# Projections with channels in rows from normed activations, and longer runs of half-array products, in a hybrid decoder layer

## The chip, the cores and the metric

The kernel runs on one core of one Trainium2 chip. The metric is device time in microseconds (us) for one execution, of the slowest core (here the only one). Times of a kernel are given as the median of several runs. One execution is recorded by the hardware profiler, and all rows of a profile come from that one.

The engines are TensorE (PE in the rows, its weight loads PEld), VectorE (DVE), ScalarE (ACT), GpSimd (POOL) and SyncE (SP), which here issues the DMAs. TensorE multiplies a stationary operand (128x128 at most) with a moving one and writes PSUM, which has eight banks of 512 fp32 columns in 128 partitions.

## The reference, cut to what matters

One decoder layer on 256 tokens of width 1024, in fp32:

```python
h = rms_norm(x, ln1_g)
q, k, v, z, xbc, dt, gate_a, gate_b = split(h @ w_in)          # 1024 -> 10272
y_a = attention(head_norm(q), head_norm(k), v) @ w_o_attn        # 16 heads of 64, causal in one block
xbc = silu(causal_conv(xbc))                                     # depthwise, 4 taps along the tokens
y   = ssd(xbc, softplus(dt + dt_bias)) + d_skip * xs             # 32 heads of 64, 4 groups, 2 chunks of 128
y_b = (group_rms_norm(y * silu(z)) * norm_g) @ w_o_ssm
x  += (sigmoid(gate_a) * y_a + sigmoid(gate_b) * y_b) @ w_out
h2  = rms_norm(x, ln2_g)
g, u = split(h2 @ w_gate_up)                                     # 2 x 2816
x  += (silu(g) * u) @ w_down
x  += (p @ w_ple_proj) * sigmoid(rms_norm(x, ln3_g) @ w_ple_gate)
```

## The kernel before, in words

**Precision.** TensorE multiplies in a format that rounds fp32 (`F32R`). Each weight tile and each activation is split into a rounded part and the rest: `wh` by ScalarE, `wl = raw - wh` by VectorE (`split_w`, L263), likewise `ah` and `al`. A product is the sum of `ah wh + ah wl + al wh`.

**Panels.** A panel is 512 output columns for all 256 tokens. `Panel.step` (L348) makes, for one slice of 128 of the inner dimension and one half of the tokens, three matmuls whose stationary operand is the activation (128 channels x 128 tokens) and whose moving operand is 512 columns of the weight. Tokens come out in the partitions, in two PSUM banks (tag `g`, four banks). A panel of inner dimension 1024 has 48 matmuls. `PANELS` lists the panels of the input projection in their order. `yb` stands for a group of the SSM's output projection (`ssm_out`, L846). The activations are `g1 * x` without the factor 1/rms; that factor, `rstd1`, is applied to each panel's result.

**After a panel.** xbc and z are wanted with channels in the partitions. `evac_xbc` (L482) and `evac_z` (L516) therefore scale the result into SBUF, transpose it with TensorE (eight 128x128 transposes for a panel, L192), and then take the convolution or the tanh. Gate and up are computed as eleven panels of 256 gate and 256 up columns; `evac_gu` (L996) takes the sigmoid and the products, and `ff_task` (L1006) transposes the result (four transposes) and splits it for the down projection.

**SSM and attention.** `ssm_task` (L591) goes through four groups of eight heads, in two units of four heads. `seg` makes the decays, `out_` (L664) the diagonal products: matmuls with 64 stationary columns, two of which run in the two halves of the array (`halves`, L176). `off` adds what the first chunk passes to the second, `ssm_finish` (L717) gates and norms. `attention_task` (L746) goes through eight pairs of heads: `scores`, `transp`, `values`.

**Residuals.** `Residual.take` (L954) adds a panel to the residual stream, transposes and splits the sum, and makes 1/rms beside that. For gate/up the 1/rms is applied at the end, in `evac_gu`.

**Order.** The order on TensorE is written out: `queue` (L156) makes every instruction follow the last main matmul, and `Filler` slips the small tasks between the steps of panels. A task says how many modelled nanoseconds it waits before its next part (`LAG`, by step). On the other engines the order follows ranks (`prio`): weights (`w`) come before evacuations (`ev`), these before the rest (`bg`). The DMAs of the weights stand on SP's queue, 512 KB each, with four raw, three `wh` and six `wl` tiles.

Of the kernel before, what the change touches and what calls it, by code (L numbers as in the profile page):

```python
# [10 lines left out]
F32 = mybir.dt.float32  # L11
# [24 lines left out]
    ('xbc', 0, 5120),  # L36
    ('xbc', 5, 7680),
    ('xbc', 1, 5632),
    ('xbc', 2, 6144),
    ('xbc', 3, 6656),  # L40
    ('k', 0, 1024),
    ('q', 0, 0),
    ('z', 0, 3072),
    ('z', 1, 3584),
    ('gb', 0, 9248),
    ('yb', 0, None),
    ('yb', 1, None),
    ('q', 1, 512),
    ('v', 0, 2048),
    ('z', 3, 4608),  # L50
    ('k', 1, 1536),
    ('z', 2, 4096),
    ('gb', 1, 9760),
    ('v', 1, 2560),
    ('yb', 2, None),
    ('yb', 3, None),
    ('ga', 1, 8736),
    ('ga', 0, 8224),
]
NFF = 11  # L60

# [5 lines left out]

LAG = {
    "dt": 9198, "dt.t": 3823, "dt.e": 24762, "dt.low": 2074, "dt.end": 6965, "xbc": 3815, "xbc.t": 1507,
    "xbc.end": 7967, "z": 7477, "z.t": 2878, "z.end": 2196, "qk": 21856, "qk.t": 1263, "qk.end": 1856,  # L70
    "v": 3215, "cb": 0, "rows": 538, "prep": 3126, "seg": 492, "seg.next": 11553, "out": 13590,
    "out.xdt": 4839, "out.end": 90, "off": 3340, "off.end": 560, "finish": 6082, "finish.ones": 3453,
    "sc": 6834, "sc.tr": 2218, "tr": 0, "tr.val": 759, "val": 2876, "val.end": 3654, "m": 1401, "res": 4378,
    "ff": 1875, "ff.end": 1668,
# [34 lines left out]
def tile_layer(ctx: ExitStack, tc: tile.TileContext, head, xk, pt, vec, w_dt, w_big, w_dn2, w_pp, out):  # L109
    nc = tc.nc  # L110

    counters = {"w": 0, "ev": 100000, "bg": 200000, "mm": 400000}
# [15 lines left out]

    def nm(s):
        uid[0] += 1  # L130
        return f"{s}_{uid[0]}"
# [4 lines left out]
    def s2(shape, dt=F32):  # L136
        return sb.tile([P] + shape, dt, tag="s2", bufs=8, name=nm("s2"))

    def tiny(shape, dt=F32):
        return sb.tile([P] + shape, dt, tag="tiny", bufs=12, name=nm("tiny"))  # L140
# [50 lines left out]
    def transpose(o, i):  # L191
        queue(nc.tensor.transpose(o, i, ident[: i.shape[0], : i.shape[0]]).ins, False)  # L192
        fill.now += 107.0


    with prio("w"):
# [7 lines left out]
        for _ in range(7):  # L204
# [3 lines left out]
        ones = const.tile([P, 1], F32, name="ones")  # L208
        nc.vector.memset(ones, 1.0)
# [45 lines left out]
    def w_tiles():  # L255
        return (sb.tile([P, 2, 512], F32, tag="raw", bufs=4, name=nm("raw")),
                sb.tile([P, 2, 512], F32R, tag="wh", bufs=3, name=nm("wh")),
                sb.tile([P, 2, 512], F32R, tag="wl", bufs=6, name=nm("wl")))

    def split_w(tiles, js=slice(0, 2)):  # L260
        raw, wh, wl = (t[:, js] for t in tiles)
# [7 lines left out]
    def load(src, nk):  # L269

        with prio("w"):
            parts = []
            for k in range(0, nk, 2):
                tiles = w_tiles()
                nc.sync.dma_start(tiles[0], src[:, k : k + 2])
                split_w(tiles)
                parts += parts_of(tiles)
        return parts

    def load_first():  # L280

        parts = [[], []]
        with prio("w"):
            load_head(x0)
            for k in (0, 2):
                tiles = [w_tiles() for _ in range(2)]
                for j in range(2):
                    if k + j:
                        load_x(k + j, 1)
                    for b in range(2):  # L290
                        load_head(tiles[b][0][:, j])
                for j in range(2):
                    split_h(k + j)
                    for b in range(2):
                        tc.keep_in_program_order(split_w(tiles[b], slice(j, j + 1)))
# [15 lines left out]
    def next_chunk():  # L311
        c = w_big[chunk_no[0]]
        chunk_no[0] += 1
        return load(c, 4)
# [12 lines left out]
    class Panel:  # L327
# [3 lines left out]
        def __init__(self, cut=False):  # L331
# [15 lines left out]

        def step(self, piece, part, act_, last):  # L348
            tt, c, ps = piece
            ah, al = act_  # L350
# [10 lines left out]
    def rstd_of(dst, ss, scale, eps=EPS):  # L361
        t = tiny([ss.shape[-1]])
        nc.vector.tensor_scalar(t, ss, scale, eps, op0=ALU.mult, op1=ALU.add)  # L363
# [4 lines left out]
    rstd1 = const.tile([P, 2], F32, name="rstd1")  # L368
    hrstd1 = const.tile([P, 2], F32, name="hrstd1")
    eps1 = const.tile([P, 2], F32, name="eps1")  # L370

    def x_stats():
        with prio("bg"):
# [12 lines left out]
            nc.vector.tensor_scalar(hrstd1, rstd1, 0.5, None, op0=ALU.mult)  # L386

# [11 lines left out]
    def dt_task():  # L399
# [7 lines left out]
        yield fill.now + LAG["dt"]  # L407
# [12 lines left out]
        yield fill.now + LAG["dt.t"]  # L420
        with prio("bg"):
            pt_ = pb([512])
            u = tiny([2, 32])
# [6 lines left out]
            e = tiny([2, 32])  # L430
            stt(e, u, -1.0, u, op0=ALU.mult, op1=ALU.max)
            act(e, e, AF.Exp, scale=-1.0)
            s = tiny([2, 32])
# [3 lines left out]
            sq = tiny([2, 32])  # L437
            nc.vector.tensor_mul(sq, s, s)
            pol = tiny([2, 32])
# [7 lines left out]
            ea = tiny([32])  # L447
            act(ea, v[:, V_AL : V_AL + 32], AF.Exp)
            af = tiny([2, 32])
# [4 lines left out]
        yield fill.now + LAG["dt.e"]  # L454
        with prio("bg"):
# [7 lines left out]
            low = tiny([2, 32])  # L463
            nc.vector.tensor_scalar(low, pe[:, 0:2], -80.0, 80.0, op0=ALU.max, op1=ALU.min)
            el = tiny([2, 32])
# [4 lines left out]
        yield fill.now + LAG["dt.low"]  # L470
# [5 lines left out]
        yield fill.now + LAG["dt.end"]  # L476
# [3 lines left out]
    xsT, zsT, bc, qk_t, v_of, gates = {}, {}, {}, {}, {}, {}  # L480

    def evac_xbc(i, pan):  # L482
# [6 lines left out]
        yield fill.now + LAG["xbc"]  # L489
        c = s4([4, T])  # L490
        for jj in range(2):
            with prio("bg"):
# [4 lines left out]
                for j in range(2):  # L497
                    ct = 4 * i + 2 * jj + j
                    cw = [v[:, V_CW + 4 * ct + m : V_CW + 4 * ct + m + 1] for m in range(4)]
                    cc = c[:, 2 * jj + j]  # L500
                    act(cc, pu[:, j], AF.Identity, scale=cw[3], bias=v[:, V_CB + ct : V_CB + ct + 1])
                    for sft in (1, 2, 3):
                        stt(cc[:, sft:], pu[:, j, : T - sft], cw[3 - sft], cc[:, sft:], op0=ALU.mult, op1=ALU.add)  # L503
            yield fill.now + LAG["xbc.t"]
        with prio("bg"):

            th = s4([4, T])
            act(th, c, AF.Tanh, scale=0.5)
# [609 lines left out]
```

## Time and profile before

| | us |
|---|---|
| median of 3 runs (601.69 to 602.17) | 602.16 |
| the profiled execution, whole | 601.78 |
| its span, first to last instruction | 600.0 |
| PE busy | 593.8 |
| PE weight loads busy | 484.2 |
| DVE busy | 423.7 |
| ACT busy | 338.5 |
| POOL busy | 38.5 |
| input projection with SSM and attention, to the first `w_o_attn` panel | about 332 |
| gate and up, eleven panels | about 391 to 519 |

Busy times can overlap between engines. A row of the groups gives line, engine, operation, output and inputs by name, shapes, the count, then the busy time in us, the mean of one in ns, and the idle time before. L170 is the helper through which all matmuls go, L192 that of the transposes, L151 that of ACT's operations; so the operands' names tell them apart. `g` is a PSUM tile of a panel, `pb` one of the small tasks, `s` any tile in SBUF. A matmul's duration in a row contains its way through the array and overlaps with the next one.

### The profile page before, as it was taken

The page shows a single profiled execution, that of the slowest core. Times are in us where ns is not written, and L with a number is a line of the kernel's source. Part 1 is how long each engine was busy: PE and PEld are TensorE (multiplying, and loading weights), DVE is VectorE, ACT ScalarE, POOL GpSimd, SP SyncE. Part 2 cuts the span into 40 slices and gives each one's busy share as a digit, 9 for nine tenths or more (in the row PEclk, how much of TensorE's full clock was granted, in tenths as well). Part 3 has the DMA queues.
Part 4 walks back from the last instruction along what each step waited for, and adds up shares of the span by engine and source line. Part 5 has one row for each costly group of instructions (what it writes and reads, how often), then busy time and mean ns, then how long its engine had stood idle before and what let it go on. Part 6 is the DMA issues. An engine that isn't in the chain of part 4 may idle for free.

```text
span 600.0 us, 8135 instructions
## 1 busy us (share of the span) xinstructions
PE 593.8 (99%) x2961; PEld 484.2 (81%) x2961; DVE 423.7 (71%) x667; ACT 338.5 (56%) x512; POOL 38.5 (6%) x47
## 2 busy tenths in 40 slices
PE   9999999999999999999999999999999999999997
PEld 7888888787777878887777788888888888888886
DVE  5689999978997765677865575756756666646465
ACT  6766666556774545476646444755544544445353
POOL 2000103412010111101000000000000000000000
PEclk9999999999999999999999999999999999999999
DMA  8845644543444445655555475556555565555641
GB/s 303 320 141 167 208 143 142 176 137 113 138 135 144 143 156 162 194 167 158 160 159 163 140 234 186 186 165 203 170 202 185 163 202 189 184 188 183 196 147 70
DMA packets 31048, 103.88 MB, mean 173 GB/s; under 512 B 3552, under 2 KB 4640, under 8 KB 31008
## 3 DMA queue, kind: packets, MB, share of 16 engines
q1 hardware_dynamic: 31008, 103.36, 53.3%
q8 instruction: 23, 0.38, 0.3%
q14 instruction: 17, 0.14, 0.1%
HBM read 102.23 MB, written 1.05 MB: 172 GB/s over the span
## 4 chain that ended last, share of the span: by engine, by line
PE 97%; DVE 1%; ACT 0%; DMA 0%; issue 0%; SPq 0%; ACTq 0%
PE g L170 85%; PE pb L170 6%; PE pb L192 5%; DMA raw<-in_head 0%; DVE s L733 0%; ACT wh L151 0%; DVE s L641 0%; ACT s L151 0%; DVE wl L263 0%; DVE s L768 0%; DVE s L646 0%; DVE s L725 0%; DVE s L1043 0%; DVE s L1044 0%; DVE s L765 0%
## 5 line engine op out<-in xcount | busy, mean ns | idle before, releaser
L170 PE MATMUL g<-wh,s 128*128 128x512 f32 x1504 | 486.7, 395 | 0.1
L170 PEld LDWEIGHTS g<-wh,s 128*128 128x128 f32 x1504 | 282.1, 188 | 59.1 <-issue 1.9
L263 DVE TENSOR_TENSOR wl<-raw,wh 128x1024 fp32r<-128x1024 f32 (+1 forms) x192 | 230.2, 1201 | 130.3 <-ACT wh L151 128.0
L151 ACT ACTIVATE wh<-raw 128x1024 fp32r<-128x1024 f32 (+1 forms) x192 | 199.7, 1042 | 176.2 <-PE g L170 151.6
L170 PE MATMUL g<-wl,s 128*128 128x512 f32 x752 | 294.8, 392 | 0.0
L170 PEld LDWEIGHTS g<-wl,s 128*128 128x128 f32 x752 | 141.6, 188 | 28.2 <-issue 1.0
L151 ACT ACTIVATE s<-pb 128x512 f32<-128x512 f32 (+4 forms) x64 | 33.6, 543 | 30.6 <-PE pb L192 16.1
L192 PEld LDWEIGHTS pb<-ident,s 128*128 128x128 f32 x302 | 37.9, 140 | 11.4 <-issue 0.9
L192 PE MATMUL pb<-ident,s 128*128 128x128 f32 x302 | 47.1, 272 | 0.0
L151 ACT ACTIVATE s<-g,rstd 128x512 f32<-128x512 f32 (+1 forms) x50 | 28.5, 583 | 20.8 <-PE g L170 19.1
L503 DVE SCALAR_TENSOR_TENSOR s<-pb,vecs,s 128x255 f32<-128x255 f32 (+2 forms) x72 | 32.0, 474 | 1.8 <-ACT s L151 1.6
L170 PE MATMUL pb<-s,s 128*64 128x128 f32 (+6 forms) x328 | 32.6, 304 | 0.4 <-ACT s L151 0.4
L151 ACT ACTIVATE s<-pb,vecs 128x256 f32<-128x256 f32 (+2 forms) x48 | 25.9, 549 | 10.9 <-PE pb L192 5.0
L170 PEld LDWEIGHTS pb<-s,s 128*64 128x64 f32 (+2 forms) x328 | 23.1, 154 | 9.9 <-issue 4.7
L364 POOL TENSOR_TENSOR rstd<-tiny,mhalf 128x2 f32<-128x2 f32 x3 | 2.3, 762 | 314.4 <-DVE tiny L363 295.3
L151 ACT ACTIVATE s<-s 128x512 f32<-128x512 f32 (+3 forms) x24 | 19.0, 792 | 5.0 <-DVE s L958 4.0
L554 POOL TENSOR_TENSOR tiny<-tiny,mhalf 128x8 f32<-128x8 f32 x8 | 16.0, 1994 | 73.2 <-DVE tiny L552 73.2
L618 POOL TENSOR_SCALAR_AFFINE_SELECT rr<-a_h 128x512 fp32r<-128x512 f32 x16 | 13.6, 860 | 100.7 <-PE pb L170 56.9
L151 ACT ACTIVATE s<-s,tiny 128x128 f32<-128x128 f32 (+1 forms) x32 | 14.2, 445 | 6.4 <-DVE tiny L771 6.4
L1002 DVE SCALAR_TENSOR_TENSOR s<-g,rstd,s 128x256 f32<-128x256 f32 x22 | 10.6, 481 | 7.5 <-ACT s L151 7.5
L659 DVE TENSOR_TENSOR s<-s,s 128x512 f32<-128x512 f32 x16 | 11.9, 747 | 0.3 <-ACT s L151 0.3
L1003 DVE SCALAR_TENSOR_TENSOR s<-g,rstd,s 128x256 f32<-128x256 f32 x22 | 10.6, 484 | 0.7
(120 smaller groups left out, 235.6 us busy)
## 6 DMA issues: line engine op xcount, KB each, us to landing
raw<-in_w_big SPq DMA_DIRECT2D x176, 512.0 KB
raw<-in_head SPq DMA_DIRECT2D x8, 256.0 KB
raw<-in_head SPq DMA_DIRECT2D x4, 512.0 KB
s<-in_xk SPq DMA_DIRECT2D x4, 512.0 KB
raw<-in_w_pp SPq DMA_DIRECT2D x2, 512.0 KB
raw<-in_w_dn SPq DMA_DIRECT2D x2, 512.0 KB
out<-s SPq DMA_DIRECT2D x3, 256.0 KB
xraw<-in_head SPq DMA_DIRECT2D x2, 256.0 KB
```

The source lines that it names most:

```text
L151: return nc.scalar.activation(o, i, f, **kw)
L170: ins = nc.tensor.matmul(o, lhsT, rhs, start=start, stop=stop).ins
L192: queue(nc.tensor.transpose(o, i, ident[: i.shape[0], : i.shape[0]]).ins, False)
L263: nc.vector.tensor_sub(wl, raw, wh.bitcast(F32))
L364: nc.gpsimd.tensor_tensor(dst, t, mhalf[:, : ss.shape[-1]], op=ALU.pow)
L503: stt(cc[:, sft:], pu[:, j, : T - sft], cw[3 - sft], cc[:, sft:], op0=ALU.mult, op1=ALU.add)
L554: nc.gpsimd.tensor_tensor(f, ms, mhalf, op=ALU.pow)
L618: nc.gpsimd.affine_select(r, bcast(a_h[:, c, h0 : h0 + 4].bitcast(F32), P), pattern=[[0, 4], [1, P]], compare_op=ALU.is_ge, fill=0.0, base ...
L659: nc.vector.tensor_tensor(m, m, cbm[:, g, c].unsqueeze(1).to_broadcast([P, 4, P]), op=ALU.mult)
L1002: stt(t[:, tt], pan.ps[tt][:, :T], r, t[:, tt], op0=ALU.mult, op1=ALU.mult)
L1003: stt(t[:, tt], pan.ps[tt][:, T:], r, t[:, tt], op0=ALU.mult, op1=ALU.mult)
```

## The change

- **Channels in rows.** From the sixth panel on (`NORMED`), xbc and z panels (`BY_ROWS`, eight of them) and all of gate/up make the weight the stationary operand and the activations the moving one, so that channels come out in the partitions. *Narrow* blocks take three matmuls with 256 columns, *wide* ones (`WIDE`, and all of gate/up) take one with 512 columns, `wh` against `[ah | al]`, and one with 256, `wl` against `ah`; their two halves are then added. The weights' layout in memory follows.
- **Normed activations.** `norm_rows` makes `g1 * x / rms` once and splits it again; 1/rms is spread over the partitions by a product of ones and a diagonal matrix. Panels from the sixth on need no factor after them.
- **Residual before gate/up.** The sum is scaled by 1/rms before it is transposed and split; these steps have the new highest rank (`hot`), and the transposes stand between the products of the p projection.
- **Runs of half-array products.** `out_` takes all eight heads of a group in one run; three of the four value products of attention follow directly on the next pair's scores.
- **The start.** The first weight load is two halves; `open` orders the first products by what is there; one warming product fewer.
- **Also.** Another panel order; a waiting time for each single use of a step; four `wh` and five `wl` tiles, more small tiles; the group norm's sum over channels by transposes and ACT's accumulator; small steps of 1/rms on POOL.

```diff
 PANELS = [
-    xbc4 xbc0 xbc5 xbc1 xbc2 xbc3 k0 q0 z0 z1 gb0 yb0 yb1 q1 v0 z3 k1 z2 gb1 v1 yb2 yb3 ga1 ga0
+    xbc4 xbc0 k0 gb0 v0 xbc5 q0 xbc1 z0 xbc2 z3 xbc3 z1 yb0 q1 k1 yb1 z2 v1 yb2 ga1 gb1 ga0 yb3
 ]
+NORMED = 5
+BY_ROWS = [kind in ('xbc', 'z') and n >= NORMED for n, (kind, _, _) in enumerate(PANELS)]
+WIDE = [('z', 0), ('z', 1), ('z', 2), ('xbc', 5), ('xbc', 3)]
...
+    def rows_step(ps, tiles, k, acts_, wide):
+        wh, wl = (x.rearrange("p a n -> p (a n)")[:, k * P : k * P + P] for x in tiles[1:])
+        ah, al, both = acts_[k]
+        if wide:
+            if k == 7:
+                mm(ps[:, :T], wl, ah, False, False, main=True)
+            mm(ps, wh, both, k == 0, k == 7, main=True)
+            if k < 7:
+                mm(ps[:, :T], wl, ah, False, False, main=True)
+        else:
+            mm(ps, wh, ah, k == 0, False, main=True)
+            mm(ps, wh, al, False, False, main=True)
+            mm(ps, wl, ah, False, k == 7, main=True)
+        fill.step()
...
+    def norm_rows():
+            pr = pb([T])
+            mm(pr, ones, rdiag.rearrange("p a t -> p (a t)"), True, True)
+            for k in range(0, 8, 2):
+                h32 = s2([2, T])
+                both = s4([2, 2, T], F32R)
+                for j in range(2):
+                    stt(h32[:, j], xk_, g1[:, k + j : k + j + 1], pr, op0=ALU.mult, op1=ALU.mult)
+                act(both[:, :, 0], h32)
+                nc.vector.tensor_sub(both[:, :, 1], h32, both[:, :, 0].bitcast(F32))
...
+                    for k in range(8):
+                        rows_step(ps if wide else ps[:, j], w, k, h_n, wide)
+                    if wide:
+                            act(u[:, j], ps[:, T:])
+                            nc.vector.tensor_add(u[:, j], ps[:, :T], u[:, j])
+                evac_rows(kind, i, jj, u if wide else ps, to)
...
-        def out_(g, qd):
-                yds = [pb([2, P]) for _ in range(2)]
+        def out_(g):
+                yds = [pb([2, 2, P]) for _ in range(2)]
                 halves(
-                    for j in range(2) for c in range(2) for hf in range(2))
+                    for qd in (1, 0) for j in range(2) for c in range(2) for hf in range(2))
...
-        def scores(p):
+        def scores(p, also=None):
+                vals, finish = values(*also) if also else ([], None)
-                halves(
+                halves([
-                    for hf in range(2))
+                    for hf in (1, 0)] + vals)
...
 class Residual, take:
-            fill.spawn(split_t(...), 0)
+            if not self.normed:
+                fill.spawn(split_t(...), 0)
-            with prio("bg"):
+            with prio("hot" if self.normed and n == 1 else "bg"):
                     act(junk, b[:, tt], AF.Square, accum_out=self.ss[:, tt, n : n + 1])
+                        nc.gpsimd.tensor_add(sss, self.ss[:, tt, 0:1], self.ss[:, tt, 1:2])
+                        rstd_of(self.dst[:, tt : tt + 1], sss, 1.0 / 1024, on=nc.gpsimd)
+                            scaled = act(self.toks[nn][tt], self.base[nn][:, tt], scale=self.dst[:, tt : tt + 1])
...
+                pan.step(pc, parts[k], (p_h[:, k], p_l[:, k]), k == 1)
+                if 4 * n + 2 * tt + k >= 4:
+                    res2.split(*ready.pop(0))
...
+    def gate_up(n, pg, pu):
+            act(u[:, 0], pg[:, T:])
+            nc.vector.tensor_add(u[:, 0], pg[:, :T], u[:, 0])
+            act(f[:, 0], u[:, 0], AF.Sigmoid)
+            nc.vector.tensor_mul(f[:, 0], f[:, 0], u[:, 0])
+            act(u[:, 1], pu[:, T:])
+            nc.vector.tensor_add(u[:, 1], pu[:, :T], u[:, 1])
+            nc.vector.tensor_mul(f[:, 0], f[:, 0], u[:, 1])
+            act(fh, f[:, 0])
+            nc.vector.tensor_sub(fl, f[:, 0], fh.bitcast(F32))
+    for n in range(2 * NFF):
+        tiles = load_tiles(next_src(), 4, None if n else res2.scaled)
+        pss = [psg.tile([P, 512], F32, tag="g", name=nm("g")) for _ in range(2)]
+            for ps, w in zip(pss, tiles):
+                for k in range(8):
+                    rows_step(ps, w, k, h2, True)
+        gate_up(n, *pss)
```

More of the change, by code (lines that the diff above doesn't have):

```diff
@@ L189, in mm3, with transpose @@
         mm(o, ll, rh, False, stop)
-    def transpose(o, i):
-        queue(nc.tensor.transpose(o, i, ident[: i.shape[0], : i.shape[0]]).ins, False)
+    def transpose(o, i, main=False):
+        queue(nc.tensor.transpose(o, i, ident[: i.shape[0], : i.shape[0]]).ins, main)
         fill.now += 107.0
@@ L275, in load, with cuts @@
                 nc.sync.dma_start(tiles[0], src[:, k : k + 2])
-                split_w(tiles)
-                parts += parts_of(tiles)
-        return parts
+                rounded = split_w(tiles)
+                if behind is not None and k + 2 == nk:
+                    follow(rounded.ins, behind)
+                yield tiles
+    def load(src, nk):
+        return [part for tiles in load_tiles(src, nk) for part in parts_of(tiles)]
+    def cuts(k, b):
+        return [WHOLE] if k or b else HALVES
     def load_first():
@@ L488, in evac_xbc @@
                 tok.append(t)
-        yield fill.now + LAG["xbc"]
+        yield fill.now + lag("xbc")
         c = s4([4, T])
@@ new lines, in evac_xbc, with evac_rows, end_rows @@
+            yield fill.now + lag("xbc.t")
+        yield from silu_xbc(i, c)
+    def evac_rows(kind, i, jj, ps, to):
+        with prio("ev"):
+            if kind == "xbc":
+                conv(i, to, jj, ps)
+            else:
+                zz = to[:, 2 * jj : 2 * jj + 2]
+                act(zz, ps, AF.Tanh, scale=0.5)
+                stt(zz, zz, 1.0, ps, op0=ALU.add, op1=ALU.mult)
+    def end_rows(kind, i, to):
+        if kind == "xbc":
+            yield from silu_xbc(i, to)
+        else:
+            yield fill.now + lag("z.end")
+            zsT[i] = to
@@ L813, in values, with finish, wait_values @@
                     prods += [(pa[rows_of[hf], i, P:T], vt[:, 1, cols[hf]], t1[:, hf], False, True) for hf in range(2)]
-                halves(prods)
-                act(ah, pa)
-                nc.vector.tensor_sub(al, pa, ah.bitcast(F32))
-        for n in range(10):
+            def finish():
+                with prio("bg"):
+                    act(ah, pa)
+                    nc.vector.tensor_sub(al, pa, ah.bitcast(F32))
+            return prods, finish
+        def wait_values(p):
+            while p[0] not in v_of:
+                yield fill.now + 500
+            yield tm["t", p] + lag("tr.val")
+        for n in range(9):
             if n < 8:
```

472 lines of the change are left out of this document (273 added, 199 removed).

## The prediction

> **What bounds the kernel now.** I read the page's busy times, its slices and its chain first. They say which engine sets the end.
>
> ```profile
> span 600.0 us, 8135 instructions
> PE 593.8 (99%) x2961; PEld 484.2 (81%) x2961; DVE 423.7 (71%) x667; ACT 338.5 (56%) x512; POOL 38.5 (6%) x47
> ...
> PE   9999999999999999999999999999999999999997
> DVE  5689999978997765677865575756756666646465
> ...
> PEclk9999999999999999999999999999999999999999
> ...
> PE 97%; DVE 1%; ACT 0%; DMA 0%; issue 0%; SPq 0%; ACTq 0%
> ```
>
> TensorE (PE) is busy in every slice and makes 97% of the chain that ends last, at the full granted clock. So the time is the sum of what PE issues, plus its few waits, plus the head and the tail. What is removed from PE's stream counts in full, as long as no other engine becomes late. VectorE (DVE) is at 9 tenths or more from the fourth slice on, so it is the engine to watch.
>
> A busy PE is not a price, because matmuls overlap. The price is the pace, and it stands in the chain of waits in order of time (start, duration, what; the 0.44 us row is four transposes, the last row the end of the kernel):
>
> ```profile
> 480.18 4.11 PE g L170 x18
> 484.29 0.22 PE pb L192 x2
> 484.51 6.83 PE g L170 x30
> 491.35 0.22 PE pb L192 x2
> ...
> 578.12 0.44 PE pb L192 x4
> ...
> 594.26 1.45 PE pb L170 x12
> ```
>
> The first four rows are one gate/up panel: 4.11 + 0.22 + 6.83 + 0.22 = 11.38 us, 48 matmuls of 128x512 and 4 transposes. A matmul with 512 moving columns takes 6.83/30 = 0.2277 us, a transpose 0.11 us. The twelve of the last row are the cut panel's, with 256 moving columns, as the groups by shape say (count; busy us, mean ns; idle), the last two for the stretch from 594 us:
>
> ```profile
> L192 PE MATMUL pb<-ident,s 128*128 128x128 f32 x300 | 46.8, 272 | 0.0
> ...
> L170 PE MATMUL pb<-wh,s 128*128 128x256 f32 x8 | 1.6, 282 | 0.0
> L170 PE MATMUL pb<-wl,s 128*128 128x256 f32 x4 | 1.1, 283 | 0.0
> ```
>
> They take 1.45/12 = 0.1208 us each, with a weight load of their own each. Half the columns cost 53% of the time, so a matmul costs about 0.2138 us per 512 columns and 0.0139 us for itself.
>
> **The change part by part.**
>
> *Transposes out.* Eight of the xbc and z panels (BY_ROWS) and all of gate/up now come out with channels in the partitions, which is what the transposes made before. A panel of xbc or z had 8 transposes, a gate/up panel 4: 8x8 + 11x4 = 108 of the 300. At 0.11 us: **-11.9 us**.
>
> *More, smaller matmuls.* The columns streamed stay the same: per 128 channels and slice of K, 768. Before they came as 1.5 matmuls of 512. A wide panel takes one of 512 (wh against both halves of the activations) and one of 256 (wl): 0.3485 us against 0.3416. A narrow one takes three of 256: 0.3624 us. Gate/up has 22x2x8 = 352 such pairs: 352 x 0.0069 = 2.4 us. Five wide xbc/z panels have 160: 1.1 us. Three narrow ones have 96: 96 x 0.0208 = 2.0 us. Together **+5.5 us** for 400 more matmuls. The bounds are 0 (the fixed part hides) and 8.1 (the 800 matmuls of 256 at half of 0.2277 plus twice the 0.0069 found); I take the pace measured, because in the cut panel these same shapes follow each other.
>
> The Trainium skill ("TensorE: Matmul & The Clock Gate", Back-to-back issue gap) gives a warm gap of N/2.4 + 2.5 ns, so 216 ns and 109 ns. By it the 400 extra matmuls cost an estimated 1.0 us and the change would end some 4.5 us lower. This trace has 0.2277 and 0.1208 us, so the measurement decides and the sum keeps 5.5.
>
> *One run for eight heads.* The half-array products of a group's SSM diagonal (`out_`) come as one run of 32 records where there were two of 16, and three of the four value products of attention follow the next scores directly. That is 4 + 3 fewer switches. The chain of waits prices runs of both kinds:
>
> ```profile
> 141.23 1.02 PE pb L170 x16
> ...
> 304.55 0.89 PE pb L170 x12
> ```
>
> If the difference of these rows is taken for 4 records, 0.13 us, then 12 cost 0.39 and 0.50 us would be fixed. The forms differ, so that is an upper end. The lower end is 0. I take 0.15 us: 7 x 0.15 = **-1.0 us** (0 to -3.5).
>
> *Normed rows.* `norm_rows` puts one fp32 product of 256 columns on PE (two records, so about as much as four of the transposes): **+0.4 us**. Its 8 multiply-multiplies and 4 splits on DVE lie under two panels (gb 0, v 0: 2 x 10.9 us) that still take the old activations. The four SSM sums become two transposes each for two fp32 products with one column: counted at 0 (-0.2 to 0.2).
>
> *The head.* The first weight load is cut in two and the first products are ordered by what is there. The chain's first pieces, and one row of ACT's timeline:
>
> ```profile
> 1.25 2.64 DMA raw<-in_head
> 3.89 0.02 issue
> 3.91 0.64 ACT wh L151
> 4.55 0.04 issue
> 4.59 22.86 PE g L170 x96
> ...
> 3.04 0.51 ACT L151 ACTIVATE s<-x 128x256 fp32r<-128x256 f32 x1 [0.75 <-DMA x<-in_head]
> ```
>
> The first matmul at 4.59 waits for 256 KB and a rounding of 0.64 us. It cannot start before the activations are rounded (3.55) and a half of the weights behind them (about 0.4): 3.95, so 0.6 us earlier. The 96 matmuls take 22.86 us where 96 x 0.2277 = 21.86 are due: another 1.0 us of waiting for the subtraction, of which the new order covers some with products that need only wh. Bounds 0.6 and 1.6; I take **-1.0 us**. One DMA more on SP's queue costs its issue alone.
>
> *The residual before gate/up.* This is what the change makes worse. Before, the scale 1/rms was applied at the end of gate/up, so nothing waited for it. Now the rows are scaled before they are transposed, and gate/up's first matmul is behind: add, square, three small steps on POOL, ACT's scaling, transposes, split. The same steps before, from the timeline by engine (the add on DVE, square and its sum on ACT, the power on POOL):
>
> ```profile
> 379.28 0.69 DVE L958 TENSOR_TENSOR s<-g,s 128x512 f32<-128x512 f32 x1 [2.03 <-PE g L170]
> ...
> 380.64 0.62 ACT L151 ACTIVATE s<-s 128x512 f32<-128x512 f32 x1
> 381.16 0.19 ACT L151 ACTIVATION_READ_ACCUMULATOR s<-s 128x1 f32 x1
> ...
> 383.25 0.70 POOL L364 TENSOR_TENSOR rstd<-tiny,mhalf 128x2 f32<-128x2 f32 x1 [103.73 <-DVE tiny L363]
> ```
>
> Laid end to end: 0.69 + 0.62 + 0.19 + 0.70, two more POOL steps (0.1 to 0.7 each; I take 0.3), a scaling like the square (0.62) and some 0.3 of hand-overs give 3.7 us. The cover until the first of these transposes stands at PE's head is 15 matmuls of the p projection, 3.4 us. What stands behind that transpose on PE is the rest of the projection and gate/up itself. Before, the power came 3.97 us after the add began, because a weight rounding (1.06 us) and splits lay between. The "hot" rank moves these steps ahead, but one instruction already running cannot be passed: the wait is 0.3 to 2.5 us, I take **+1.0 us**. After that each split's ACT work (2 x 0.47) is shorter than the 1.39 us in which two slices of K are used, so nothing else is late.
>
> *Waits that stand now.* The busy time of each engine by stage (length; PE, weight loads, DVE, ACT, POOL; clock, DMA):
>
> ```profile
> 29.00:63.00 34.00, 34.00 (x166) 27.74 (x165) 30.10 (x67) 22.48 (x33) 0.00 (x0) 1.00 0.53 163
> 63.00:168.00 105.00, 104.64 (x562) 84.53 (x561) 95.12 (x171) 67.36 (x106) 21.59 (x20) 1.00 0.46 149
> 168.00:206.00 38.00, 37.66 (x228) 29.94 (x227) 31.41 (x62) 22.47 (x49) 1.91 (x3) 1.00 0.43 136
> 206.00:332.00 126.00, 126.00 (x656) 101.42 (x656) 87.00 (x143) 73.22 (x118) 9.22 (x6) 1.00 0.51 162
> ...
> 391.00:519.00 128.00, 128.00 (x585) 105.06 (x584) 81.84 (x101) 64.07 (x78) 0.00 (x0) 1.00 0.57 184
> ```
>
> From 63 to 206 PE is idle 0.70 us. The new order gives the SSM groups more room (yb 0 stands five panels after z 0 instead of three, yb 1 four after z 1 instead of three): **-0.4 us** (-0.7 to 0, apart from the rival below).
>
> *DVE and ACT, at nothing while covered.* Gate/up has ten DVE operations per former panel in place of five. Groups by shape (count; busy us, mean ns; idle before):
>
> ```profile
> L263 DVE TENSOR_TENSOR wl<-raw,wh 128x1024 fp32r<-128x1024 f32 x184 | 224.8, 1223 | 128.1 <-ACT wh L151 125.8
> ...
> L1003 DVE SCALAR_TENSOR_TENSOR s<-g,rstd,s 128x256 f32<-128x256 f32 x22 | 10.6, 484 | 0.7
> ...
> L727 DVE TENSOR_TENSOR s<-s 128x256 f32<-128x256 f32 x4 | 1.7, 416 | 0.0
> ```
>
> A block of 128 lasts 16 x 0.3485 = 5.58 us and needs two weight subtractions (2.45) and five operations of 0.42 to 0.48 (2.1 to 2.4): 4.6 to 4.9 us. DVE goes from 64% to about 85% there and hides; without cover it would cost up to 22 x 2.4 us. The pair's two PSUM tiles come free one block ahead of their next use.
>
> The sum: -11.9 + 5.5 - 1.0 + 0.4 - 1.0 + 1.0 - 0.4 = **-7.4 us**. The profiled execution took 601.78 us, 1.78 around its span, so 594.4; by the median of 602.16 it is 594.8. I forecast 594.4.
>
> **The rivals.**
>
> *DVE becomes the bound from 29 to 206 us* (the slower side). It is busy 30.10 + 95.12 + 31.41 = 156.6 of 177 us now. The same stretch gains 16 additions of wide panels (6.7 to 7.7), `norm_rows` (8 x 0.48 + 4 x 0.69 = 6.6) and z 3, which comes earlier (1.4): 171.5. PE's part shrinks by about 4 to 173. If DVE can hold no more than the 91% of 63 to 168, it needs 188 us: +15, the time is 609. It decides once this demand passes PE's stretch. For it: the 99% that come out. Against: from 206 to 332 DVE has 39 us free, and what is put off there (attention, later SSM groups) has later panels to meet; PE lost only 0.36 us beside a DVE at 91%.
>
> *The gain is part given back.* The residual chain waits 2.5 us, and weight subtractions arrive late in the dense stretch a few times (0.4 us each, as the idle now): 3 to 5 us back, about 598.5. For it: one slow instruction in an ordered queue is enough. Against: the weight tiles run several ahead.
>
> *More gain.* The switches cost 0.5 each, the head gives 1.6, no wait at the residual: 3.5 + 0.6 + 1.0 more than forecast less what the idle keeps, about 589.8.
>
> *The transposes filled waits.* If PE would wait for its next weights anyway, taking the fillers out saves nothing: 601.8 and the added matmuls up to +5. Against: the stretch 391 to 519 has no idle, and the 0.2277 pace is the same on both sides of a transpose.
>
> **How the numbers follow.** A measurement of this kernel tells 0.2% (1.2 us) from no change. Forecast (592 to 597) 0.58; given back (597 to 600.9) 0.17; more gain 0.12; fillers 0.05, mostly no change; DVE bound 0.08, slower. So faster 0.87, same 0.05, slower 0.08. The range 589.5 to 600 leaves out the slow case, the fillers and the ends of the others.
>
> **What would show it.** Transposes 192 instead of 300, plus 8 for the SSM sums. Gate/up at 11.15 us per former panel. Pairs at 0.348 us; if they pace at 0.36 or more, the matmul term was too small. PE idle under 3 us after the first matmul; a gap behind the last w_out panel is the residual chain. DVE near 95% from 29 to 206 with PE idle there would be the slow rival. An end above 600 or a PE idle of more than 6 us makes the prediction wrong.

## The result, and the profile after

The changed kernel takes **593.4 us** (median of 4 runs, 593.17 to 593.84) where the kernel before, timed beside it, takes 602.16 us (601.69 to 604.25). The ratio is 0.985, with a 95% interval from 0.983 to 0.987. The profiled execution took 593.17 us, 1.67 around its span; the prediction had 594.4.

The page of the changed kernel, its parts 1, 2 and 4:

```profile
span 591.5 us, 8951 instructions
PE 584.0 (99%) x3251; PEld 494.9 (84%) x3251; DVE 450.5 (76%) x752; ACT 347.0 (59%) x592; POOL 47.0 (8%) x62
...
PE   8999999999999999999999999999999999999997
...
DVE  5789999999999879888556765777777777546464
...
PEclk9999999999999999999999999999999999999999
...
PE 96%; DMA 1%; ACT 1%; issue 1%; DVE 0%; SPq 0%; POOL 0%; ACTq 0%; DVEq 0%
```

PE still sets the end, at the full granted clock. DVE has moved: it is at 9 tenths or more from the fourth slice to the thirteenth without a break. The groups by shape (count; busy us, mean ns; idle before):

```profile
L212 PE MATMUL g<-wh,s 128*128 128x512 f32 x876 | 282.2, 395 | 0.7 <-ACT wh L193 0.7
...
L212 PE MATMUL g<-s,wh 128*128 128x512 f32 x512 | 177.7, 399 | 1.1 <-DVE s L1068 1.1
...
L212 PE MATMUL g<-s,wl 128*128 128x256 f32 x608 | 161.1, 282 | 0.0
...
L234 PE MATMUL pb<-ident,s 128*128 128x128 f32 x200 | 29.4, 273 | 0.0
```

There are 200 transposes, 512 wide pairs (one product of 512 and one of 256) and, in the row of 608, 96 products of 256 that belong to the narrow panels. PE's idle time on panel products is two pieces: 0.7 us in the head, for a weight rounding, and 1.1 us for a split of the residual. The busy times by stretch of the changed kernel (length; PE, weight loads, DVE, ACT, POOL; clock, DMA):

```profile
63.00:168.00 105.00, 105.00 (x741) 94.53 (x740) 100.16 (x194) 68.08 (x128) 16.49 (x16) 1.00 0.50 162
168.00:206.00 38.00, 38.00 (x209) 31.36 (x208) 36.07 (x62) 26.34 (x48) 9.22 (x7) 1.00 0.47 149
...
380.00:503.00 123.00, 123.00 (x700) 106.99 (x699) 93.19 (x156) 72.12 (x132) 0.00 (x0) 1.00 0.59 189
```

From 63 to 206 us PE has no idle left (0.70 us before), while DVE is busy 95% of it. In gate/up DVE is at 76%.

Where the time went, by the starts of each stretch's first product on PE (worked out from the two traces, us):

```
                                  before    after    difference
start of the first panel product    4.59     3.89      -0.70
from there to w_o of attention    327.73   320.90      -6.83
w_o of attention                   23.98    22.68      -1.30
w_out                              22.91    22.71      -0.20
p projection and gate/up          132.02   132.92      +0.90
w_down                             61.29    60.81      -0.48
the last two products' panels      22.90    22.87      -0.03
```

The gain comes ahead of w_out: 8.83 us. The stretch with gate/up, the largest edit of the change, has become no shorter; the 0.48 us of w_down are four transposes that the last gate/up panel used to leave there.

### The profile page after: what moved, and what is told of

Its sections match the earlier page's. It is cut to its first block, busy times and chain, and to the rows that moved or that the text cites. A ratio compares the mean times of both kernels' runs of the same rounds, so it can differ in the third digit from the quotient of the medians.

```text
span 591.5 us, 8951 instructions
## 1 busy us (share of the span) xinstructions
PE 584.0 (99%) x3251; PEld 494.9 (84%) x3251; DVE 450.5 (76%) x752; ACT 347.0 (59%) x592; POOL 47.0 (8%) x62
## 4 chain that ended last, share of the span: by engine, by line
PE 96%; DMA 1%; ACT 1%; issue 1%; DVE 0%; SPq 0%; POOL 0%; ACTq 0%; DVEq 0%
PE g L212 87%; PE pb L212 6%; PE pb L234 3%; DMA raw<-in_head 1%; ACT s L193 0%; SPq L288 0%; ACT wh L193 0%; DVE s L1122 0%; DVE wl L303 0%; POOL rstd L430 0%; DVE s L1068 0%; DVE s L1236 0%; DVE s L1237 0%; POOL tiny L1131 0%; POOL tiny L429 0%
## 5 line engine op out<-in xcount | busy, mean ns | idle before, releaser
L303 DVE TENSOR_TENSOR wl<-raw,wh 128x1024 fp32r<-128x1024 f32 (+2 forms) x193 | 230.7, 1199 | 109.0 <-ACT wh L193 108.1
L193 ACT ACTIVATE wh<-raw 128x1024 fp32r<-128x1024 f32 (+2 forms) x193 | 199.6, 1037 | 175.1 <-PE g L212 88.8
L212 PE MATMUL g<-wh,s 128*128 128x512 f32 (+1 forms) x900 | 287.2, 392 | 0.7 <-ACT wh L193 0.7
L212 PE MATMUL g<-s,wh 128*128 128x512 f32 (+1 forms) x704 | 214.2, 369 | 1.1 <-DVE s L1068 1.1
L212 PEld LDWEIGHTS g<-wh,s 128*128 128x128 f32 x900 | 168.2, 188 | 35.9 <-issue 1.3
L212 PE MATMUL g<-wl,s 128*128 128x512 f32 (+1 forms) x450 | 173.4, 388 | 0.0
L212 PE MATMUL g<-s,wl 128*128 128x256 f32 x608 | 161.1, 282 | 0.0
L212 PEld LDWEIGHTS g<-s,wh 128*128 128x128 f32 x704 | 122.5, 189 | 19.7 <-DVE s L1068 1.4
L212 PEld LDWEIGHTS g<-s,wl 128*128 128x128 f32 x608 | 114.9, 189 | 5.9
L212 PEld LDWEIGHTS g<-wl,s 128*128 128x128 f32 x450 | 84.4, 188 | 16.6 <-issue 0.5
```

Source lines behind the costliest of these rows:

```text
L193: return nc.scalar.activation(o, i, f, **kw)
L212: ins = nc.tensor.matmul(o, lhsT, rhs, start=start, stop=stop).ins
L303: nc.vector.tensor_sub(wl, raw, wh.bitcast(F32))
```

## The experiments

Each is the changed kernel with the edit shown, unless it says otherwise. Times are medians with their lowest and highest run; the ratio is to the kernel before, timed beside it.

**Gate/up back in columns.** The loop of the kernel before, with 1/rms behind gate/up:

```diff
-    res2 = Residual(xin, V_G2, rstd2, True)
+    res2 = Residual(xin, V_G2, rstd2, False)
-    for n in range(2 * NFF):
-        (two blocks of 128 channels, rows_step, gate_up)
+    for n in range(NFF):
+        (one panel of 512 columns, 4 transposes, 1/rms at its end)
```

> The changed kernel with gate/up back in columns as before: activations stationary, 44 transposes, 1/rms applied after the products, so no chain ahead of gate/up's first matmul. The sum as predicted (rows save 4.8 us of transposes, cost 2.4 in matmuls and 1.0 in waiting): 1.4 us slower than the changed kernel, 594.8. The reading of the two traces (p projection and gate/up together 132.0 us before, 132.9 after, since a pair of row matmuls paces at 0.352 and PE idles some 1.7 us at the residual): 0.9 us faster, 592.5.

Measured: 593.6 us (592.78 to 594.42), ratio 0.985 (0.983 to 0.988). Rows in gate/up bring nothing that can be measured here. What 44 transposes save goes into the pace of the pairs and the wait in front, both below.

**Four later xbc panels back in columns.**

```diff
-BY_ROWS = [kind in ('xbc', 'z') and n >= NORMED ...]
+BY_ROWS = [kind == 'z' and n >= NORMED ...]
```

> The changed kernel with the four later xbc panels in columns from the normed rows: 8 groups of four transposes back (8 x 0.44 = +3.5 us), fewer matmuls (two wide panels 0.7, two narrow ones 1.3 less), 8 additions of 0.42 us less on DVE. If PE's sum sets the time: +1.5 us, 594.9. If DVE is the bound in the dense stretch: not slower, 593.4 or 1 to 3 us under it.

Measured: 605.49 us (604.91 to 606.37), ratio 1.006 (1.004 to 1.007): 12 us more than the changed kernel, where 32 transposes make up 3.5. Behind the head PE stands 6.7 us in this run and 1.1 us in the changed kernel. The longest wait in PE's timeline:

```profile
183.12 1.14 PE L234 MATMUL pb<-ident,s 128*128 128x128 f32 x6
187.95 0.80 PE L212 MATMUL g<-wh,s 128*128 128x512 f32 x1 [3.69 <-DVE s L1037]
188.54 0.63 PE L212 MATMUL g<-wl,s 128*128 128x512 f32 x1
188.97 1.05 PE L212 MATMUL g<-wh,s 128*128 128x512 f32 x2
```

PE stands 3.69 us, and the products behind it start 0.43 us apart in place of 0.23. The PSUM bank that it waits for is freed by the wide addition (L1037) of a panel ahead, which comes late on DVE's queue. With waiting times that were set for rows, the new order runs into such stops when xbc comes in columns. New waiting times were not tried, so the run does not show that rows are needed.

**Only the new order, in the kernel before** (its waiting times unchanged):

```diff
 (the kernel before)
-PANELS = [ (order before) ]
+PANELS = [ (order after) ]
```

> The kernel before with only the new panel order (all panels in columns, old waiting times). If the order only takes away idle time: 0.4 to 1 us faster than before, 601.2 to 601.8. If the order makes much of the gain: 598 or less. If it needs the new waiting times: slower than before.

Measured: 622.91 us (622.42 to 623.55), ratio 1.034 (1.032 to 1.036). PE's timeline, and the busy times of the stretch behind:

```profile
277.94 0.95 PE L170 MATMUL pb<-s,s 64*128 64x128 f32 x12
284.15 0.79 PE L170 MATMUL g<-wh,s 128*128 128x512 f32 x1 [5.26 <-ACT s L151]
```

```profile
285.00:300.00 15.00, 15.00 (x71) 11.87 (x70) 9.96 (x28) 7.80 (x23) 1.39 (x2) 0.81 0.13 42
```

This is the longest of several waits, 11.5 us in all behind the head (0.7 us in the kernel before); behind it stand 15 us at a granted clock of 0.81. With the waiting times of before, the new order is a loss.

**The old order, with everything else of the change.** Only five of the panels then come in rows; waiting times that run out are repeated.

```diff
-PANELS = [ (order after) ]
+PANELS = [ (order before) ]
```

> The changed kernel with the order of panels from before (waiting times that run out are repeated); nothing is left out. Only five of the xbc and z panels are then behind the normalization and come in rows (xbc 3 and the four of z), three more stay in columns and have 24 transposes more (2.6 us) and 1.6 us less of smaller matmuls. Theory 'order and rows go together': the groups of the SSM become ready early and crowd VectorE, PE waits for PSUM banks as it does with the new order alone in the old kernel, and the time is 600 us or more. Rival 'the rows bring the gain, the order is a detail': 593.4 + 2.6 - 1.6 + 0.4 to 1.5 of waits as in the kernel before, 594.5 to 596.

Measured: 627.82 us (626.94 to 628.28), ratio 1.043 (1.041 to 1.044), far beyond what I expected. PE's timeline, and the busy times by stretch:

```profile
115.62 1.08 PE L212 MATMUL pb<-rr,gt_r 128*128 128x512 f32 x4
125.79 0.77 PE L212 MATMUL g<-s,wh 128*128 128x512 f32 x1 [9.08 <-DVE s L630]
```

```profile
100.00:115.00 15.00, 15.00 (x70) 12.42 (x69) 15.00 (x28) 7.70 (x9) 0.00 (x0) 1.00 0.56 185
115.00:130.00 15.00, 5.92 (x23) 4.71 (x22) 11.41 (x15) 5.44 (x10) 9.04 (x6) 0.66 0.28 93
```

The q and k panels stand together just ahead of the first z panel. DVE is full for 15 us before; the q and k results sit in their PSUM banks until their norms have gone through DVE and POOL (L630 is the last step), and the z panel in rows, which takes a bank for each 128 channels, gets none for 9 us. A second stop of 7.70 us, at 80.7 us, ends behind the last step of xbc's silu on DVE (L570); in all PE stands 23.6 us behind the head. So the old order and the rows do not go together with these waiting times. Both order experiments run with waiting times that were set for another sequence; how much of the 21 and 34 us a new set would take back was not tried.

**More work on DVE.** 16 additions of 128x512, whose results nobody uses, one behind each `evac_rows` half:

```diff
+            nc.vector.tensor_add(s2([2, T]), to[:, 2 * jj : 2 * jj + 2], to[:, 2 * jj : 2 * jj + 2])
```

> The changed kernel with one more addition of 128x512 (about 0.69 us on DVE) after each half of the eight row panels, 16 in all, 11 us of DVE between 63 and about 240 us; its result is not used. If DVE has room there: under 1 us slower, 593.4 to 594.4. If DVE is the bound there: 8 to 11 us slower, 601 to 604.

Measured: 604.42 us (603.21 to 604.82), ratio 1.003 (1.002 to 1.004): 11.0 us more for 16 x 0.69 = 11.0 us of DVE. That the two figures are equal is chance: PE does not wait once for each addition, but in a few places. The chain of waits of this run, then PE's timeline and the busy times of that stretch:

```profile
108.11 1.13 DVE wl L303
109.24 0.85 DVE s L563 x3
...
110.32 0.86 DVE s L563 x2
111.19 1.13 DVE wl L303
112.32 0.79 DVE s L563 x2
...
113.25 3.54 PE g L212 x10
```

```profile
109.03 0.39 PE L212 MATMUL g<-s,wh 128*128 128x512 f32 x1
113.25 0.76 PE L212 MATMUL g<-s,wh 128*128 128x512 f32 x1 [3.83 <-DVE s L563]
...
114.02 0.63 PE L212 MATMUL g<-s,wh 128*128 128x512 f32 x1
...
114.66 0.63 PE L212 MATMUL g<-s,wh 128*128 128x512 f32 x1
```

```profile
105.00:120.00 15.00, 11.17 (x51) 9.60 (x50) 14.30 (x27) 6.73 (x11) 1.17 (x2) 0.77 0.32 107
```

The convolution (L563) reads the panel out of PSUM in several steps on DVE, between weight subtractions; its bank comes free late, PE stands 3.83 us, and then a pair takes 0.64 us instead of 0.352 for 5.7 us, at a granted clock of 0.77 over this stretch. Behind the head PE stands 8.3 us where it stood 1.1, and the half pace costs about 2.9 us more. In the order as written, DVE has no room for this work between 63 and 206 us. Here too the waiting times stayed.

**Less work on DVE.** The five wide xbc and z panels as narrow ones: 20 additions and 20 copies fewer, and 160 products of 512 become 320 of 256.

```diff
-WIDE = [('z', 0), ('z', 1), ('z', 2), ('xbc', 5), ('xbc', 3)]
+WIDE = []
```

> The changed kernel with the five wide xbc and z panels done as narrow ones: three matmuls of 256 columns for each 128 channels and slice of K in place of one of 512 and one of 256, so 160 pairs at 0.360 us in place of 0.352 (+1.3 us on PE), and 20 additions of 128x256 on VectorE (about 8 us) and 20 copies on ScalarE fewer. Nothing is left out. Theory 'PE's own pace sets the time, VectorE is just covered': 594.4 to 594.9, since work taken from VectorE buys nothing where PE is never idle. Rival 'VectorE is the edge that sets the pace of the stretch from 63 to 206 us too': the 8 us taken away are worth more than PE's 1.3 us, time 590 to 593.

Measured: 594.65 us (594.37 to 595.21), ratio 0.988 (0.986 to 0.989): 1.25 us more, PE's 1.3 us. The busy times by stretch:

```profile
63.00:168.00 105.00, 105.00 (x842) 99.70 (x841) 96.10 (x184) 63.92 (x115) 17.23 (x16) 1.00 0.48 161
168.00:206.00 38.00, 38.00 (x231) 32.49 (x230) 33.05 (x56) 25.06 (x44) 5.87 (x7) 1.00 0.43 146
```

DVE has 4.1 and 3.0 us less, and PE, never idle in either kernel, is no faster for it. The two runs together put the changed kernel at the edge: 11 us more on DVE cost PE several stops, 7 us less bring nothing.

**Without 1/rms ahead of gate/up.** The rows are split unscaled; the factor 1/rms of the second normalization is left out of the result.

```diff
-                            scaled = act(self.toks[nn][tt], self.base[nn][:, tt], scale=self.dst[:, tt : tt + 1])
+                    self.toks = [[self.base[nn][:, tt] for tt in range(2)] for nn in range(2)]
```

> The changed kernel without the factor 1/rms ahead of gate/up (left out of the computation): the residual's sum is transposed and split at once, nothing on PE waits for the square, the three POOL steps and the four scalings. If that chain is what PE waits for between the p projection and gate/up: that stage falls from 132.9 to 131.3 us, 591.8 in all. If the two weight roundings on ACT (2.0 us) and subtractions on DVE (2.4 us) ahead of the splits set the wait: at most 0.5 us less.

Measured: 591.84 us (591.26 to 592.8), ratio 0.984 (0.982 to 0.985); p projection and gate/up together take 131.22 us, 1.7 less than 132.92. That is what the scaling costs in this place, with ACT's wait for the power. One rounding of a weight tile, which in the changed kernel has to follow the scaling, comes free with it.

**The SSM diagonal in two runs per group, value products apart from the scores.**

```diff
+            for qd in (1, 0):
                 halves(... for j in range(2) for c in range(2) for hf in range(2))
-                scores(pairs[n], also)
+                scores(pairs[n]); (then the values in a run of their own)
```

> The changed kernel with the SSM diagonal of a group in two runs of half-array products with main matmuls between them, and the three value products apart from the scores: seven switches more. By the prediction 7 x 0.15 = 1.0 us slower, 594.4. By the pace between records in the two traces (half-array products and what enters them, 1.5 us less after): 1.5 us, 594.9. If the ordered queues are so full that any shift lets something be late: 3 us or more.

Measured: 595.02 us (594.63 to 595.84), ratio 0.989 (0.987 to 0.991), 1.6 us more than the changed kernel. The chain of waits of the changed kernel, where eight heads are one run, and of this one:

```profile
208.67 1.90 PE pb L212 x32
```

```profile
211.16 1.02 PE pb L212 x16
...
213.08 1.02 PE pb L212 x16
```

The run itself gains 2 x 1.02 - 1.90 = 0.14 us. The rest lies in the panel products around it: in both traces the last product ahead of such a run takes 0.09 us longer than its neighbours (0.318 against 0.227 us from start to start), and the first one behind it 0.11 us longer.

**The first weight load in one piece.** The order of the first products stays.

```diff
-        return [WHOLE] if k or b else HALVES
+        return [WHOLE]
```

> The changed kernel with the first weight load in one piece of 256 KB, as before; the new order of the first products stays. By the prediction the cut is worth about 0.6 of the head's 1.0 us: 594.0. By the traces the loads behind are what PE waits for (it starts 0.7 us earlier and stands 0.9 us at the fifth load): the same, 593.4, or up to 0.5 us faster.

Measured: 595.08 us (594.88 to 595.53), ratio 0.989 (0.988 to 0.990), 1.7 us more. The heads by the chain of waits, this kernel first, the changed kernel behind it:

```profile
4.58 23.93 PE g L212 x96
28.51 1.87 PE pb L212 x16
```

```profile
3.13 4.32 DMA raw<-in_head
...
8.15 19.34 PE g L212 x84
27.49 1.87 PE pb L212 x16
```

In the changed kernel the first product starts at 3.89, but behind the product at 7.0 PE loses 0.9 us (0.75 of them idle) to the weights that land at 7.45, and the dt product comes at 27.49: where it came before the change too (4.59 + 22.86 = 27.45). Without the cut it comes at 28.51. There PE stands 0.51 us ahead of the first product, and the products run at half pace (0.43 us) until 8.6 us:

```profile
4.58 2.07 PE L212 MATMUL g<-wh,s 128*128 128x512 f32 x4 [0.51 <-ACT wh L193]
```

In the trace of before, with one warming product more, PE stands 0.10 us there and the half pace lasts until 5.9 us. So the run does not separate the cut from the missing warming product. The head also differs between executions: in the traces of this section that share the changed kernel's head the dt product comes between 27.2 and 28.4 us, and with the head of before it came at 27.45 in one trace and, in the run with only the new order, at 29.87. The 1.7 us rest on the medians; one profile of each does not explain them.

**The second half of the scaling behind gate/up's first products.**

```diff
+                if 4 * n + 2 * tt + k == 5:
+                    res2.scale(1)
+                if k < 2:
+                    res2.split(*ready.pop(0))
```

> The changed kernel with the second half of the residual (its scaling, transposes and splits) moved behind the first two inner slices of gate/up, so that ACT reaches the first half's splits earlier. If ACT's and DVE's queues set the wait there: the stage falls by 0.8 to 1.4 us, 592.0 to 592.6. If the chain to 1/rms sets it: no change.

Measured: 595.04 us (594.04 to 595.78), ratio 0.989 (0.987 to 0.990). PE's wait in front of gate/up is 2.01 us here, and the two stretches take 134.0. The scaling was not the last link: two weight roundings still stood ahead of the splits on ACT. That led to the last two.

**The roundings behind the splits.** First, gate/up's second and third weight tile are rounded behind the first and second split:

```diff
-                if behind is not None and k + 2 == nk:
-                    follow(rounded.ins, behind)
+                if behind is not None and behind[k // 2] is not None:
+                    follow(rounded.ins, behind[k // 2])
-        tiles = load_tiles(next_src(), 4, None if n else res2.scaled)
+        tiles = load_tiles(next_src(), 4, ([None, rounded[0]], [rounded[1], None])[n] if n < 2 else None)
```

> The changed kernel, with the roundings of gate/up's second, third and later first weight tiles on ScalarE made to follow the first two splits of the second normalization in place of its scaling. Nothing is left out. In the changed kernel ScalarE does the last scaling until 375.07 us, then two roundings of 1.99 us, and the splits from 376.96, while the transposes of the first split stand ready from 374.4; PE then waits 1.13 us at 378.95 and 0.2 to 0.6 us in small pieces. Theory 'the two roundings and their two subtractions in front of the splits are the wait': the splits begin near 375.1, the wait behind the projection falls to 0.4 us or less, gate/up's second tile comes at most 0.3 us late, the stretch from the last w_out panel to the end of gate/up falls by 1.0 to 1.5 us, time 592.0 to 592.5. Rival 'the wait moves on to the weights': the second tile's rounding now ends after gate/up has begun and PE waits there for as long: 593.0 to 593.8. Rival 'the rows' own chain of square, power and scaling is what is late': no change, 593.4.

Measured: 592.75 us (592.15 to 593.32), ratio 0.984 (0.983 to 0.986). The projection's stretch fell by 1.37 us, gate/up's grew by 0.58 in five small gaps. Then the third tile's rounding went behind the last split:

```diff
-        ... ([None, rounded[0]], [rounded[1], None]) ...
+        ... ([None, rounded[0]], [rounded[3], None]) ...
```

> The changed kernel with the rounding of gate/up's second weight tile behind the first split of the second normalization, and that of its third tile behind the fourth and last split (with the third tile behind the second split, the wait of 1.1 us in front of gate/up was gone, the stretch of the projection fell by 1.37 us, and five gaps of 0.1 us each between 378 and 383 us gave 0.58 us back, while roundings and splits took turns). Nothing is left out. Theory 'the roundings between the splits make those gaps': without the third tile's there the splits keep pace with 1.4 us of products for two slices, gate/up takes 124.2 us, projection and gate/up together 131.6 to 131.7 us (132.9 in the changed kernel), time 592.0 to 592.5. Rival 'each split is late by itself, or the third tile is late now': 132.1 or more together, 592.6 to 593.4.

Measured: **591.64 us** (591.47 to 592.1), ratio 0.982 (0.980 to 0.984); the two stretches take 131.48 us. ACT's timeline in the changed kernel and in this one, from the end of the scaling on (start, duration, what):

```profile
375.07 1.99 ACT L193 ACTIVATE wh<-raw 128x1024 fp32r<-128x1024 f32 x2
376.96 2.27 ACT L193 ACTIVATE s<-pb,vecs 128x256 fp32r<-128x256 f32 x6
```

```profile
375.00 0.81 ACT L194 ACTIVATE s<-pb,vecs 128x256 fp32r<-128x256 f32 x2
375.71 1.05 ACT L194 ACTIVATE wh<-raw 128x1024 fp32r<-128x1024 f32 x1
376.66 2.29 ACT L194 ACTIVATE s<-pb,vecs 128x256 fp32r<-128x256 f32 x6
```

The splits begin 1.96 us earlier and the wait is gone: in this kernel's chain the transposes end at 377.76 and 127 products follow without a break.

```profile
377.32 0.44 PE pb L235 x4
377.76 22.25 PE g L213 x127
```

This version is below both kernels; nothing else in it differs.

## Why the prediction was right, and where not

The terms, with what the traces and runs gave:

| term | predicted | measured | from |
|---|---|---|---|
| 108 transposes out | -11.9 | -12.2 | 64 ahead of w_out -7.3, with the longer first product behind each run; 44 in gate/up at 0.11 |
| smaller matmuls | +5.5 | +7.0 | +3.2 for xbc and z, +3.8 in gate/up |
| longer half-array runs | -1.0 | -1.6 to -2.1 | the run with them apart; the two traces |
| normed rows | +0.4 | +0.4 | trace |
| SSM sums as transposes | 0 | -1.0 | trace |
| head | -1.0 | 0 | dt product at 27.45 and 27.49, one execution each |
| residual ahead of gate/up | +1.0 | +1.4 | run with the roundings behind the splits |
| waits that stood | -0.4 | -0.8 | 0.70 us from 63 to 206 us, 0.10 ahead of the first product |
| not in the sum | 0 | -1.2 | other small SSM products -1.0, w_out -0.2 |

The measured column adds to -8.5 (with -2.1 for the runs); the profiled executions differ by 601.78 - 593.17 = 8.61. The trace figures are sums of the times from one start on PE to the next, by kind of instruction. The mechanism was the one I named: PE hardly idles, so what leaves its stream counts in full. The 1.2 us by which the forecast lies above the profiled execution is what is left of errors in both directions: 2.9 us too little gain ahead of w_out (-5.9 there by the terms, -8.8 measured) and 1.6 too much from there on (-1.4 and +0.2). That they nearly cancel is luck. Of the signs named, the 200 transposes, PE's idle time (0.7 + 1.1 us, under 3) and the gap ahead of gate/up came as written.

**The SSM sums** were "counted at 0", with bounds of 0.2, and left their bounds by 0.8. A row of the groups before has the 16 records of products with a single column:

```profile
L170 PE MATMUL pb<-ones,s 128*128 128x1 f32 x16 | 2.1, 235 | 0.3 <-DVE s L727 0.3
```

From start to start they took 1.69 us, and some 0.25 us more in the products on both sides; the wait of 0.3 us in this row is counted with the waits. The eight transposes cost 0.9 with the products behind them. I set two transposes against two fp32 products as equal, without a row for it; a record with one column takes 0.1 us, like a transpose, and each such product is two records.

**The pair's pace** is the term that was off by most, 1.4 us. I took 0.3485 us from products whose moving side is the weights. In the changed kernel the activations move. PE's timeline of it shows seven pairs from the first of these rows to the last, 2.47 us:

```profile
379.41 0.39 PE L212 MATMUL g<-s,wh 128*128 128x512 f32 x1
379.64 0.28 PE L212 MATMUL g<-s,wl 128*128 128x256 f32 x1
...
381.88 0.40 PE L212 MATMUL g<-s,wh 128*128 128x512 f32 x1
```

That is 0.353 a pair, and 0.352 over the rest of gate/up. The product of 512 columns takes 0.235 where it took 0.2277, the one of 256 takes 0.117 where it took 0.1208. Over 352 pairs that is 1.4 us on a term of 2.4, and gate/up took 124.15 / 11 = 11.29 us per former panel instead of the 11.15 named. With the residual's wait it ate the whole gain of gate/up: -4.8 + 3.8 + 1.4 = +0.4, which is the +0.9 of the stretch less the 0.48 of the four transposes that lay in w_down. By the formula of the Trainium skill for the gap ("TensorE: Matmul & The Clock Gate", Back-to-back issue gap), an estimated 216 and 109 ns, the gaps come out below the measured ones again; the sum by them would have been further off in gate/up. The upper bound of the matmul term, 8.1, does not follow from its own working, which gives 800 x 0.0138 = 11.0; the 7.0 measured lie under both.

**Half-array runs**: 0.15 us a switch was too low, -1.6 us for 7 is 0.23. I had compared the runs' own rows; most of the price lies in the panel products on both sides.

**The residual**: the bounds of 0.3 to 2.5 held, but the cause I gave, that "one instruction already running cannot be passed", was not the one. Two roundings that were ready first stood ahead of the splits in ACT's queue, and their subtractions on DVE; two ordering edges moved them.

**The head**: the start came 0.7 us earlier, as worked out, but the second half of the step failed: the third weight tile lands at 7.45 us where its rounding began at 6.12 before, and PE loses 0.9 us to it. Against the same kernel with a whole first load the changed head is still worth 1.7 us. Why the early half pace lasts longer in one execution than in another stays open.

**The rivals.** That VectorE becomes the bound did not happen, but its step failed too: I let DVE hold 91% at most, and it held 95% with PE never idle; demand came to 31.24 (29 to 63 us) + 100.16 + 36.07 = 167.5 us where I had 171.5. In gate/up it was busy 76%, where I had 85%. The prediction also read DVE's slices of before too high: they are at 9 tenths in the fourth to eighth and in two more, not "from the fourth slice on". 11 us of added work were enough to stop PE. And it bites by another door than the one I argued, which was weights subtracted late: what comes late is the PSUM bank of the panel before, which I had costed at nothing. That the transposes filled waits fell: 1.3 us of added products cost 1.25 us. Waits gave gain back at the residual and, 0.75 us idle, in the head; the rest of what gate/up lost is the pair's pace.

## What to carry to other kernels

Where the matrix engine never idles, price every instruction by the time from its start to the next start, and include the neighbours: a switch of form, a product with one column and a slower form of product cost between about 0.01 and 0.23 us each and decided here over several microseconds. Before adding work to an engine at 95%, test its slack in both directions with dummy and removed work; the page's busy share does not say on which side of the edge it stands. And look for what stands ahead of a late link in its own queue before shortening the link: two ordering edges took 1.4 us out of the stretch here, where moving half of the scaling added 1.1.

## What the runs showed of the hardware that I had not expected

A wait of PE can cost more than its length. Behind waits of 3.69, 3.83, 5.26 and 9.08 us the products ran at half pace, for 5.7 us where more work lay on DVE, and the clock row of these stretches shows 0.66 to 0.81; behind the wait of 1.1 us at the residual, and behind that of 2.01 us in the run with the late half, the pace was full at once. A single long wait is not needed, though. With only the new order in the kernel before, no wait from 195.0 to 198.4 us is longer than 0.79 us, but PE is busy only 1.92 of these 3.4 us, and in the next 3.4 us the granted clock is 0.50. So idle time spread over a stretch can do it too; no run places the threshold. By the Trainium skill ("TensorE: Matmul & The Clock Gate", What's actually happening) at least one idle window of about 3.4 us halves the clock, at least one busy window of about the same length brings it back, and the window runs on its own, whatever the kernel does. The 5.7 us fit that, between one window and two; the stretch at 195 us shows that the first window need not be idle throughout.

In the head the pace is halved too (0.43 us until 8.6 us in the run with the whole load), while the clock row of that stretch shows 1.00:

```profile
3.00:9.00 6.00, 5.49 (x17) 4.28 (x16) 3.78 (x7) 4.28 (x8) 1.26 (x5) 1.00 1.00 345
```

The row counts a stretch without a clock record as full, and the first record of this trace begins at 8.6 us, just where the half pace ends (6.0 in the kernel before, 4.4 in the changed one). So the clock row does not show the slow start; the distance of the starts does. In the traces that share the changed kernel's head the first record begins anywhere from 4.2 to 7.3 us: the end of the slow start differs from one execution to the next.

And a product of 512 columns is 7 ns slower with activations as the moving side than with weights (0.235 against 0.2277). One of 256 is not: in the narrow panels, with activations moving, it takes 0.120, as with weights moving in the cut panel (0.1208). So the moving side alone does not make the difference; no run tells what does.
